# Hyena convolutions: 1024-wide pipelined combinations, the context's parts spread over the layer, and the Fourier products inside the second inverse transform

## The chip, the cores and the metric

The kernel runs on one core of one Trainium2 chip. The metric is the time of one execution on the device in microseconds (us), the median of several runs. Engines are named as in the profile: PE is the matrix engine (TensorE), DVE VectorE, ACT ScalarE, POOL GpSimd, SP the engine whose queue issues most loads.

## The reference

Two layers of a diffusion backbone over 1024 latent tokens and 256 context tokens, width 1024, in float32. Every layer ends with a gated FFN, and each part is modulated by six vectors per layer (shift, scale and gate, twice) that come from the conditioning vectors by `silu(cond) @ ada_w + ada_b`. Layer 1 is neighbourhood attention; layer 0 is the mixer that the change is about:

```
def mixer_ab(u, ...):                       # 1024 latent tokens, and again 256 context tokens
    p = u @ w_in                            # 1024 -> 2048 columns
    y_f = fourier_mix(p[..., :512])         # real part of a 2-D FFT in 4 groups of 128 channels
    y_h = hyena_mix(p[..., 512:], ...)
    return concatenate([y_f, y_h], -1) @ w_out

def hyena_mix(p, ...):
    z = short_conv(p, conv_w, conv_b)       # 3 taps
    x1, x2, v = split(z, 3)                 # 512 channels each
    v = x1 * long_conv(v, filt[:, 0], skip[0])
    v = x2 * long_conv(v, filt[:, 1], skip[1])
    return v                                # long_conv: rfft of length 2L, product, irfft, + skip
```

Both branches run for the latent tokens and for the context tokens with the same weights.

## The kernel before, in words

All matrices are multiplied in a split form: an operand is rounded to a 32-bit matrix format, `hi`, by ACT (`split`, L326), DVE forms the rest, `lo = x - hi` (L328), and three products, hi x hi, lo x hi and hi x lo, are added up in PSUM. So each tile that DVE or PE made costs a copy on ACT and a subtraction on DVE before PE can use it. Programs are written as Python generators that are advanced by hand (`next`), and a scheduler turns what they emit into one in-order queue for each engine. Buffers come from rotating pools: `S4` (128x1024), `S2`, `T`, `TK` and `G` (128x512), in PSUM `PS` (six banks) and `PQ` (two). In the profile `S4` and `S2` tiles are called `s`, the pools `T`, `TK`, `G` are `t`, `tk`, `g`, the banks `ps` and `pq`, matrices of the transforms `mat` (loaded as `cs`), DRAM scratch `d`.

Layer 0 goes through these stages:

- `in_proj` (L821) multiplies by `w_in` in 16 blocks. Between its blocks run `ada_group` (six modulation vectors; here m = 2 to 5, two steps per block, on DVE at L507) and the transforms of the context's filters.
- `turned` (L932) transposes the latent operand into eight blocks.
- The first long convolution is eight `unit(0, fb, cls)` (L967): products with a transform matrix give two PSUM banks, the real and imaginary spectrum of 128 frequencies by 512 channels. A unit of class 0 has 12 matmuls, one of class 1 has 24, in two halves. `combine` (L904) then multiplies by the filter's spectrum: for each of the two parts DVE makes two products (L919 and L920), POOL adds or subtracts them (L921), and ACT and DVE split the sum into Y.
- `inverse_first` (L1000) transforms back in four groups of products (j, r), and DVE and POOL form from them, with the gate x1, the operands of the second convolution (L1025 to L1046).
- Eight `unit(1, fb, cls)` follow; three of them have their first halves ahead of the end of `inverse_first`. Then `inverse_last` (L1053) transforms back and applies x2.
- `fourier_l` (L1253) is the second half of the latent Fourier mix, and `out_proj` (L1338) multiplies by `w_out`.
- The context's own parts (`fourier_c`, `forward_c(0)`, `inverse_c(0)`, `forward_c(1)`, `inverse_c(1)`) form one chain, `ctx_chain`, advanced one step at a time while `inverse_first`, the units and `inverse_last` run; its products use `pq`.

Of the kernel before, what the change touches and what calls it, by code (L numbers as in the profile page):

```python
# [18 lines left out]
P = 128  # L19
D = 1024  # L20
KB = D // P
# [10 lines left out]
PAD_C, PAD_T, SLOT, SHIFT = 24, 88, 1088, 16  # L32
# [204 lines left out]
class Builder:  # L237
    def __init__(self, ctx, tc, a, out, taps=None, stop=None):
# [4 lines left out]
        self.p4 = ent(tc.tile_pool(name="p4", bufs=20))  # L243
        self.p2 = ent(tc.tile_pool(name="p2", bufs=35))
        self.pg = ent(tc.tile_pool(name="pg", bufs=4))
        self.pt = ent(tc.tile_pool(name="pt", bufs=7))
# [99 lines left out]
    def weights(self, src, w=1024, cut=False, keep=None, wide=False, load=None):  # L346
        st = self.S4() if wide else self.W("ws", "ws")
        if keep:
            hi, lo = keep
        else:  # L350
            hi, lo = self.pair3() if wide == 3 else self.pair1() if wide == 2 else self.pair2()
        (load or self.ld)(st.rearrange("p (n k) -> p n k", n=4) if cut else st[:, :w], src)
        self.split(st[:, :w], hi[:, :w], lo[:, :w])
        return hi, lo
# [466 lines left out]
    def in_proj(self, u, fill):  # L821
# [14 lines left out]
        for nb in order:  # L836
            wh, wl = self.weights(a["w_in"][nb])
            acc = self.lin(wh, wl, 0, range(KB), u, PCS)
            for g, n in fill:
                for _ in range(n):  # L840
                    next(g, None)
            if nb < 4:
# [18 lines left out]
            else:  # L861
# [11 lines left out]
                t = self.S2(F32, 256)  # L873
# [4 lines left out]

    def forward_c(self, o):
        nc, a = self.nc, self.a  # L880
        ab = self.ab["c"]
        tr = []
        for j in (0, 1):
            ps = self.PQ()
            for cb in range(4):
                nc.tensor.transpose(ps[:, cb * P:(cb + 1) * P], ab[cb][:, j * P:(j + 1) * P], self.ident)
            hi, lo = self.S2(F32R), self.S2(F32R)
# [3 lines left out]
        for cls in (0, 1):  # L891
            spec = []
            for i in (cls, 2 + cls):
                xh, xl = tr[(i + i // 2) % 2]
                mt = self.cmat(256, a["vf_c"][i, 0])
                ps = self.PQ()
# [4 lines left out]
            self.combine("c", o, cls, 0, spec)  # L901
            yield

    def combine(self, sq, o, cls, fb, spec):  # L904

        nc = self.nc
        Y = self.Y.setdefault((sq, o), {})
        d = self.frg[(sq, o, cls, fb)]
        fr, g = self.TK(), self.TK()
# [3 lines left out]
        if cls == 0 and fb == 0:  # L913
            fr2 = self.S2()
            self.ld(fr2, d[2])
        c, s = spec
        for kind, (x0, x1, op) in enumerate((((c, fr), (s, g), SUB), ((c, g), (s, fr2), ADD))):
# [4 lines left out]
            if sq == "l":  # L922
                key = (kind, cls, fb // 2)
                if key not in Y:
                    Y[key] = (self.S4(F32R), self.S4(F32R))
                hi, lo = (q[:, (fb % 2) * 512:(fb % 2) * 512 + 512] for q in Y[key])
            else:
                hi, lo = self.S2(F32R), self.S2(F32R)
                Y[(kind, cls, 0)] = (hi, lo)
            self.split(t0, hi, lo)  # L930

    def turned(self):  # L932
# [3 lines left out]
        for j in range(8):  # L936
# [6 lines left out]
            if j == 5:  # L943
                self.xrow = [self.S4() for _ in range(4)]
                self.xrev = []
                for cb in range(4):
                    x = self.xrow[cb]
                    self.ld(x, self.xd[0][cb][:, :LAT])
                    t = self.S2()
                    nc.scalar.copy(t.rearrange("p (j c) -> p j c", c=256),  # L950
                                   x.rearrange("p (j h c) -> p j h c", h=2, c=256)[:, :, 1, ::-1])
                    self.xrev.append(t)
            yield

    def turn_x(self, k):

        j, h = k // 4, k % 4
        n0 = (j, j, 4 + j, 2 + j)[h]
        ps = self.PQ()
        for cb in range(4):  # L960
            x = (self.xrev if h % 2 else self.xrow)[cb][:, n0 * P:n0 * P + P]
# [3 lines left out]
        self.xt[(j, h)] = t  # L965

    def unit(self, o, fb, cls):  # L967
# [13 lines left out]
        spec = [self.PS(), self.PS()]  # L981
# [11 lines left out]
        self.combine("l", o, cls, fb, spec)  # L993
        yield

    def y_of(self, o, i, f):
        kind, cls = (0, i) if i < 2 else (1, i - 2)
        return (q[:, (f % 2) * 512:(f % 2) * 512 + 512] for q in self.Y[("l", o)][(kind, cls, f // 2)])

    def inverse_first(self, ahead):  # L1000

        nc, a = self.nc, self.a
        V, G = nc.vector, nc.gpsimd
        new = [None] * 8
        for j in (0, 1):
# [27 lines left out]
            late = V if j else G  # L1033
            V.tensor_tensor(w0, c0, d0, ADD)
            V.tensor_tensor(d0, c0, d0, SUB)
# [4 lines left out]
            V.tensor_tensor(c0, w0, d0, ADD)  # L1040
            V.tensor_tensor(w0, w0, d0, SUB)
            late.tensor_tensor(c1, w1, d1, ADD)
            late.tensor_tensor(w1, w1, d1, SUB)
            p, q = self.TK(), self.TK()
            for k, (dst, x, y, op) in enumerate(((p, c0, c1, ADD), (c0, c0, c1, SUB), (q, w0, w1, ADD), (w0, w0, w1, SUB))):
                V.tensor_tensor(dst, x, y, op)  # L1046
                hi, lo = self.S2(F32R), self.S2(F32R)
                self.split(dst, hi, lo)
                new[(0, 4, 2, 6)[k] + j] = (hi, lo)
# [3 lines left out]
    def inverse_last(self, y):  # L1053

        nc, a = self.nc, self.a
        C, x = [], []
        for r in (0, 1):
            acc = [self.PS() for _ in range(4)]
            first = set()

            def product(cb, m, e, i, f):
                yh, yl = (q[:, cb * P:cb * P + P] for q in self.y_of(1, i, f))
                d = acc[cb][:, e * 256:e * 256 + 256]
                for k, (s, w) in enumerate(((yh, m[:, :256]), (yh, m[:, 256:]), (yl, m[:, :256]))):
                    nc.tensor.matmul(d, s, w, start=cb not in first, stop=e == 1 and i == 1 and f == 3 and k == 2,
                                     skip_group_check=True)
                    first.add(cb)

# [1393 lines left out]
```

## Time and profile before

| what | us |
|---|---|
| median of 3 runs (2949.43 to 2956.27) | 2953.89 |
| the profiled execution | 2960.39 |
| its span in the trace | 2957.4 |
| PE busy | 2832.0 |
| DVE busy | 2097.2 |
| ACT busy | 1328.6 |
| POOL busy | 528.5 |

In the profiled execution the input projection lies from about 255 to 452 us, the convolutions from there to 668, `fourier_l` to 706, and the output projection after it. A row of the profile names the source line, the engine, the operation and the tiles written and read, then how many there were, their busy time and mean length, and how long the engine stood idle ahead of them and for whom.

### The profile page before, as it was taken

To read this page: it belongs to the slowest core of one execution; us is meant where nothing else is said; L and a number is where in the kernel's file an instruction comes from. 1 tells how busy PE (TensorE), PEld (TensorE's weight loads), DVE (VectorE), ACT (ScalarE), POOL (GpSimd) and SP (SyncE) were. 2 spreads that over 40 slices of the span, in tenths; PEclk is the share of its full clock that TensorE was granted. 3 is DMA by queue.
4 is the path that set the end of the run, shared out by engine and by line. 5 is a ranking of instruction groups with operands and counts; after the bars stand their busy time and mean duration, and the time that the engine had idled before them with its cause. 6 is when DMAs were issued, how large, how long until landed. Compare 5 with 4: busy or idle time off the path is not lost. (4 is left out here: it accounts for less than half of the span.)

```text
span 2957.4 us, 44598 instructions
## 1 busy us (share of the span) xinstructions
PE 2832.0 (96%) x15704; PEld 2359.7 (80%) x15704; DVE 2097.2 (71%) x3984; ACT 1328.6 (45%) x2496; POOL 528.5 (18%) x816
## 2 busy tenths in 40 slices
PE   8899999689999999999999999999999999999998
PEld 3678888577899888888888888888877788788886
DVE  6667697676586777876877537788778967664555
ACT  4443325343455333333445326677765533333433
POOL 2112023251110111212010002233212012112000
PEclk9999999899999999999999999999999999999999
DMA  9674446275456555658885435777856266434663
GB/s 335 203 247 160 170 153 198 69 228 183 176 178 207 181 185 191 212 192 296 309 311 176 143 123 144 172 186 180 226 175 230 92 223 230 164 114 162 218 194 135
DMA packets 304813, 567.36 MB, mean 192 GB/s; under 512 B 83528, under 2 KB 130314, under 8 KB 304590
## 3 DMA queue, kind: packets, MB, share of 16 engines
q1 hardware_dynamic: 245950, 380.45, 41.2%
q0 software_dynamic: 56336, 179.87, 17.0%
q10 hardware_dynamic: 2304, 4.20, 0.4%
q8 instruction: 123, 2.02, 0.3%
q14 instruction: 100, 0.82, 0.1%
HBM read 414.44 MB, written 119.80 MB: 181 GB/s over the span
## 5 line engine op out<-in xcount | busy, mean ns | idle before, releaser
L1507 PE MATMUL ps<-s,s 128*128 128x512 f32 x1992 | 494.5, 390 | 5.1 <-DVE s L1398 1.7
L1507 PEld LDWEIGHTS ps<-s,s 128*128 128x128 f32 x1992 | 374.0, 188 | 84.5 <-ACT g L1512 2.1
L322 PE MATMUL ps<-s,wh 128*128 128x256 f32 (+1 forms) x1768 | 394.5, 329 | 2.7 <-ACT wh L326 2.7
L322 PEld LDWEIGHTS ps<-s,wh 128*128 128x128 f32 x1768 | 295.0, 190 | 37.8 <-ACT wh L326 5.1
L322 PE MATMUL pq<-s,wh 128*128 128x512 f32 (+1 forms) x984 | 300.4, 382 | 6.7 <-DVE s L1904 3.2
L326 ACT CAST wh<-ws 128x1024 fp32r<-128x1024 f32 (+1 forms) x142 | 145.8, 1028 | 307.7 <-PE ps L322 172.9
L1678 PE MATMUL ps<-s,s 128*128 128x512 f32 (+1 forms) x1000 | 259.3, 383 | 3.8 <-DVE s L328 3.7
L328 DVE TENSOR_TENSOR wl<-ws,wh 128x1024 fp32r<-128x1024 f32 (+1 forms) x142 | 170.4, 1201 | 128.7 <-ACT wh L326 124.1
L322 PE MATMUL ps<-s,wl 128*128 128x256 f32 (+1 forms) x884 | 256.7, 328 | 2.6 <-DVE wl L328 2.6
L326 ACT CAST s<-s 128x1024 fp32r<-128x1024 f32 (+2 forms) x184 | 168.4, 941 | 197.5 <-DMA s<-d 174.1
L322 PE MATMUL ps<-s,s 128*128 128x64 f16 (+3 forms) x2669 | 221.8, 236 | 18.6 <-DVE st L1976 8.5
L326 ACT CAST s<-t 128x512 fp32r<-128x512 f32 (+1 forms) x242 | 140.3, 591 | 199.9 <-PE ps L1507 65.8
L328 DVE TENSOR_TENSOR s<-t,s 128x512 fp32r<-128x512 f32 (+1 forms) x242 | 172.4, 723 | 77.0 <-ACT s L326 45.0
L328 DVE TENSOR_TENSOR s<-s,s 128x1024 fp32r<-128x1024 f32 (+2 forms) x162 | 185.0, 1176 | 58.3 <-ACT s L326 58.0
L1678 PEld LDWEIGHTS ps<-s,s 128*128 128x128 f32 x1000 | 184.6, 188 | 41.5 <-DVE s L328 5.1
L322 PE MATMUL ps<-s,mat 128*128 128x512 f32 x732 | 191.5, 411 | 25.8 <-ACT s L326 17.7
L322 PEld LDWEIGHTS pq<-s,wh 128*128 128x128 f32 x984 | 178.8, 190 | 39.8 <-DVE s L1904 5.0
L322 PEld LDWEIGHTS ps<-s,mat 128*128 128x128 f32 x732 | 142.0, 198 | 63.9 <-ACT s L326 20.2
L1507 PE MATMUL ps<-s,wh 128*128 128x512 f32 x608 | 189.4, 390 | 0.0
L322 PE MATMUL pq<-s,wl 128*128 128x512 f32 (+1 forms) x492 | 183.7, 380 | 0.0
L322 PEld LDWEIGHTS ps<-s,wl 128*128 128x128 f32 x884 | 164.2, 190 | 20.4 <-DVE wl L328 3.7
L313 POOL DMA_DIRECT2D d<-s x153 | 83.0, 544 | 391.9 <-DVE s L1356 116.5
(434 smaller groups left out, 5566.5 us busy)
## 6 DMA issues: line engine op xcount, KB each, us to landing
s<-d SPq DMA_DIRECT2D x282, 256.0 KB, 3.8
s<-in_down SPq DMA_DIRECT2D x150, 256.0 KB, 4.2
d<-s POOLq DMA_DIRECT2D x137, 256.0 KB, 2.8
d<-tk POOLq DMA_DIRECT2D x98, 256.0 KB, 3.1
s<-in_ada_w POOLq DMA_DIRECT2D x48, 512.0 KB, 4.7
g<-in_bias SPq DMA_DIRECT2D x128, 192.0 KB, 2.9
ws<-in_up SPq DMA_DIRECT2D x44, 512.0 KB, 4.2
d<-g POOLq DMA_DIRECT2D x87, 256.0 KB, 2.7
```

The lines of the kernel that those rows point to most:

```text
L313: self.last_ldr = self.nc.gpsimd.dma_start(out, in_).ins
L322: self.nc.tensor.matmul(o, l, r, start=st, stop=sp)
L326: self.last_hi = nc.scalar.copy(hi, src).ins
L328: self.last_lo = eng.tensor_tensor(lo, src, hi.bitcast(F32), SUB).ins
L1507: nc.tensor.matmul(ps, x[:, sl], y, start=first and j == 0 and x is wh and y is xh, stop=j == 3 and x is wl, skip_group_check=True)
L1678: m = nc.tensor.matmul(acc[j][:, c0:c1], x[:, sl], y[:, xs], start=first and k == 0, stop=last and k == 2, skip_group_check=True)
```

## The change

- `combine` becomes `combine_c` for the context and `combine_l` for the latent tokens. `combine_l` loads both factors as one tile of 1024 columns, makes each pair of products as one DVE operation 1024 wide (reading a PSUM bank twice), leaves the two sums on POOL, and puts the split off until the next unit's products (`parts`), 1024 wide as well.
- `fourier_c` (as `four`) and the start of the context's convolution (as `conv`) run inside `in_proj`, from its blocks 6 and 14 on. The rest of the context's chain stands at fixed places among the units and inside `inverse_last`.
- Of the modulation groups only m = 2 and 3 stay in `in_proj`, one step per block; m = 4 goes into the output projection, m = 5 into layer 0's FFN, three steps per pass.
- The units run in another order, and four instead of three have their first halves ahead.
- `inverse_first` has all its sums on DVE, in an order that finishes the first operands earlier; the gate x1 is loaded in halves (`gate_rows`).
- `fourier_l` is advanced inside `inverse_last`, whose POOL operation goes to DVE. `out_proj` takes its first four column blocks in two halves of the contraction, the Fourier half first.
- Pools: one `S4` more, one `T` less; the scratch for descriptors is halved.

PE's queue at the end of `inverse_first`. `s<-...,mat` rows into `ps` are its products, the `pq` rows are `fourier_c`'s. Before:

```order
L322 MATMUL ps_5290<-s_1231_4692,mat_5298 128x512
L322 MATMUL ps_5290<-s_1232_4693,mat_5298 128x512
L322 MATMUL ps_5290<-s_1231_4692,mat_5298 128x512 x2
L322 MATMUL pq_4923<-s_1274_4861,s_1294_4901 128x256
L322 MATMUL pq_4923<-s_1274_4861,s_1295_4902 128x256
L322 MATMUL pq_4923<-s_1274_4861,s_1294_4901 128x256
L322 MATMUL pq_4929<-s_1282_4869,s_1296_4905 128x256
L322 MATMUL pq_4929<-s_1282_4869,s_1297_4906 128x256
L322 MATMUL pq_4929<-s_1282_4869,s_1296_4905 128x256
L322 MATMUL ps_5290<-s_1232_4693,mat_5298 128x512
```

After, the last products of `inverse_first` (`ps_5234`) and the first of unit (0, 1) of the second convolution (`ps_5289`, `ps_5290`):

```order
L322 MATMUL ps_5234<-s_1261_4832,mat_5243 128x512
L322 MATMUL ps_5234<-s_1262_4833,mat_5243 128x512
L322 MATMUL ps_5234<-s_1261_4832,mat_5243 128x512
L322 MATMUL ps_5234<-s_1272_4869,mat_5243 128x512
L322 MATMUL ps_5234<-s_1273_4870,mat_5243 128x512
L322 MATMUL ps_5234<-s_1272_4869,mat_5243 128x512
L322 MATMUL ps_5289<-s_1337_5163,mat_5285 128x512
L322 MATMUL ps_5290<-s_1335_5159,mat_5287 128x512
```

The `pq` rows have left this part of the queue; they stand among the blocks of the input projection.

DVE's queue at the first combinations of the second convolution. Before, unit (0, 0) (`ps_5344`, `ps_5345`), among splits of the context's (`s_1463`, `s_1467`), and the start of unit (0, 1):

```order
L919 TENSOR_TENSOR t_5510<-ps_5344,tk_5504 128x512
L920 TENSOR_TENSOR t_5511<-ps_5345,tk_5505 128x512
L919 TENSOR_TENSOR t_5519<-ps_5344,tk_5505 128x512
L328 TENSOR_TENSOR s_1463_5486<-t_5480,s_1462_5485 128x512
L328 TENSOR_TENSOR s_1467_5495<-t_5489,s_1466_5494 128x512
L328 TENSOR_TENSOR s_1474_5516<-t_5510,s_1473_5515 128x512
L920 TENSOR_TENSOR t_5520<-ps_5345,s_1470_5508 128x512
L919 TENSOR_TENSOR t_5564<-ps_5396,tk_5560 128x512
L920 TENSOR_TENSOR t_5565<-ps_5397,tk_5561 128x512
```

After, units (0, 1), (1, 1) and (2, 1):

```order
L949 TENSOR_TENSOR s_1395_5408<-ps_5289,s_1394_5407 128x1024
L956 TENSOR_TENSOR s_1396_5409<-ps_5290,s_1394_5407 128x1024
L949 TENSOR_TENSOR s_1402_5440<-ps_5313,s_1401_5439 128x1024
L956 TENSOR_TENSOR s_1403_5441<-ps_5314,s_1401_5439 128x1024
L972 TENSOR_TENSOR s_1405_5448<-s_1395_5408,s_1404_5447 128x1024
L949 TENSOR_TENSOR s_1412_5484<-ps_5333,s_1411_5483 128x1024
L956 TENSOR_TENSOR s_1413_5485<-ps_5334,s_1411_5483 128x1024
L972 TENSOR_TENSOR s_1415_5492<-s_1402_5440,s_1414_5491 128x1024
```

A unit's four products and two splits became two and one, and a unit's split stands behind the next unit's products.

SP's queue in the second convolution's units: `d` rows into `tk` (before) or into 128x2x512 (after) are the factors, `cs` rows transform matrices. Before:

```order
L307 DMA tk_5638<-d_1167 128x512
L307 DMA tk_5639<-d_1167 128x512
L307 DMA cs_5732<-in_vi_c 128x512
L307 DMA tk_5688<-d_1318 128x512
L307 DMA tk_5689<-d_1318 128x512
L307 DMA cs_5812<-in_vfo_l 128x2048
```

After (`d_1663` is a row of `fourier_l`'s operands):

```order
L307 DMA s_1401_5439<-d_1318 128x2x512
L307 DMA s_1537_6033<-d_1663 128x512
L307 DMA cs_5495<-in_vfe_l 128x1024
L307 DMA cs_5528<-in_vfe_l 128x1024
L307 DMA cs_5638<-in_vke_l 128x2048
L307 DMA s_1411_5483<-d_1322 128x2x512
L307 DMA cs_5744<-in_vko_l 128x2048
L307 DMA s_1420_5513<-d_1163 128x2x512
L307 DMA cs_5750<-in_vko_l 128x2048
```

Each factor is one row now, and stands behind matrices of `inverse_last` (`vke`, `vko`) and operands of `fourier_l`, which were loaded later before.

The diff's core:

```
+    def combine_l(self, o, cls, fb, spec):
+        d = self.frg[("l", o, cls, fb)]
+        two = lambda t: t.rearrange("p (e c) -> p e c", e=2)
+        both = lambda t: t.unsqueeze(1).to_broadcast([P, 2, 512])
+        F, t0, t1 = self.S4(), self.S4(), self.S4()
+        self.ld(two(F), d[0:2].rearrange("e p c -> p e c"))
+        c, s = spec
+        nc.vector.tensor_tensor(two(t0), both(c), two(F), MUL)
+        ...
+            last = nc.vector.tensor_tensor(two(t1), both(s), two(F)[:, ::-1], MUL).ins
+        nc.gpsimd.tensor_tensor(t0[:, :512], t0[:, :512], t1[:, :512], SUB)
+        nc.gpsimd.tensor_tensor(t0[:, 512:], t0[:, 512:], t1[:, 512:], ADD)
+        self.parts(last)
+        self.sums_due = (o, cls, fb, t0)
+
+    def parts(self, after=None):
+        if self.sums_due is None:
+            return
+        o, cls, fb, t = self.sums_due
+        self.sums_due = None
+        hi, lo = self.S4(F32R), self.S4(F32R)
+        self.Y.setdefault(("l", o), {})[(cls, fb)] = (hi, lo)
+        self.nc.scalar.copy(hi, t)
+        with self.follow(after):
+            self.nc.vector.tensor_tensor(lo, t, hi.bitcast(F32), SUB)
 ...
     def in_proj(self, u, fill, four, conv):
 ...
+            if i > 5:
+                next(four, None)
+            if i > 13:
+                next(conv, None)
 ...
     def inverse_first(self, ahead):
 ...
-            late = V if j else G
             V.tensor_tensor(w0, c0, d0, ADD)
             V.tensor_tensor(d0, c0, d0, SUB)
-            G.tensor_tensor(w1, c1, d1, ADD)
-            G.tensor_tensor(d1, c1, d1, SUB)
-            for eng, k, w in ((V, 0, w0), (V, 2, d0), (late, 3, w1), (late, 1, d1)):
-                eng.tensor_tensor(w, w, self.xt[(j, k)], MUL)
+            V.tensor_tensor(w1, c1, d1, ADD)
+            V.tensor_tensor(d1, c1, d1, SUB)
+            for k, w in ((0, w0), (2, d0), (3, w1), (1, d1)):
+                V.tensor_tensor(w, w, self.xt[(j, k)], MUL)
 ...
+            sums(c0, c1, (w0, d0), (w1, d1), ADD, p, 0, 4)
+            sums(w0, w1, (w0, d0), (w1, d1), SUB, q, 2, 6)
 ...
+    def inverse_last(self, y, fl):
+        ...
+        next(fl)
         for r in (0, 1):
 ...
+            if r == 0:
+                next(fl)
+            else:
+                for _ in fl:
+                    yield
 ...
     def out_proj(self, wname, y, groups, h, l, m, after, fill):
+        todo = [(g, k, nb) for g, pcs in enumerate(groups)
+                for k, nb in ([(k, nb) for k in (0, 1) for nb in (0, 2)] + [(2, nb) for nb in range(4, KB)] if g == 0 else
+                              [(2, nb) for nb in range(KB)])]
 ...
-        ada = (x for m in (2, 3, 4, 5) for x in self.ada_group(0, m, (0, 1), "s2"))
+        ada = (x for m in (2, 3) for x in self.ada_group(0, m, (0, 1), "s2"))
-        self.in_proj(u, ((filt, 1), (ada, 2)))
+        self.in_proj(u, ((filt, (1,)), (ada, (1,))), fc, cc)
 ...
-        for k in range(8):
-            for _ in self.unit(0, k // 2, k % 2):
+        for k, (fb, cls) in enumerate(((0, 1), (0, 0), (1, 1), (1, 0), (2, 1), (3, 1), (2, 0), (3, 0))):
+            for _ in self.unit(0, fb, cls):
 ...
-        units = [self.unit(1, k // 2, k % 2) for k in range(8)]
-        for _ in self.inverse_first(units[:3]):
-            next(cc, None)
+        units = [self.unit(1, fb, cls, self.PQ if k == 3 else None)
+                 for k, (fb, cls) in enumerate(((0, 1), (1, 1), (2, 1), (0, 0), (1, 0), (3, 1), (2, 0), (3, 0)))]
+        for _ in range(2):
+            next(cc)
+        for _ in self.inverse_first(units[:4]):
+            pass
 ...
-        for i, _ in enumerate(self.inverse_last(y)):
-            if i % 2 == 0:
-                next(cc, None)
-            if i in (2, 6):
-                next(fl)
+        for i, _ in enumerate(self.inverse_last(y, self.fourier_l(y))):
+            next(cc, None)
 ...
-        self.out_proj("w_out", y, [(2, 0), (1,)], h, 0, 2, after1)
+        self.load_cond()
+        self.out_proj("w_out", y, [(2, 0), (1,)], h, 0, 2, after1, self.ada_group(0, 4, (0, 1), "s4"))
 ...
-    nc = _bacc.Bacc("TRN2", target_bir_lowering=False, num_devices=1, dynamic_dma_scratch_size=4096)
+    nc = _bacc.Bacc("TRN2", target_bir_lowering=False, num_devices=1, dynamic_dma_scratch_size=2048)
```

More of the change, by code (lines that the diff above doesn't have):

```diff
@@ L835, in in_proj @@
         next(front)
-        for nb in order:
+        for i, nb in enumerate(order):
             wh, wl = self.weights(a["w_in"][nb])
@@ L1050, in inverse_first, with product @@
+            sums(c0, c1, (w0, d0), (w1, d1), ADD, p, 0, 4)
+            sums(w0, w1, (w0, d0), (w1, d1), SUB, q, 2, 6)
             self.tr = new
             yield
-    def inverse_last(self, y):
+    def inverse_last(self, y, fl):
         nc, a = self.nc, self.a
-        C, x = [], []
+        V = nc.vector
+        C, x, late = [], [], []
+        def product(acc, first, cb, m, e, i, f):
+            yh, yl = (q[:, cb * P:cb * P + P] for q in self.y_of(1, i, f))
+            d = acc[cb][:, e * 256:e * 256 + 256]
+            for k, (s, w) in enumerate(((yh, m[:, :256]), (yh, m[:, 256:]), (yl, m[:, :256]))):
+                nc.tensor.matmul(d, s, w, start=cb not in first, stop=e == 1 and i == 1 and f == 3 and k == 2,
+                                 skip_group_check=True)
+                first.add(cb)
+        next(fl)
```

307 lines of the change are left out of this document (176 added, 131 removed).

## The prediction

> **What bounds the kernel now.** I read the page first, then the windows by stage, then in the stage that loses time the groups of TensorE, its waits, and the timeline of VectorE.
>
> ```profile
> PE 2832.0 (96%) x15704; PEld 2359.7 (80%) x15704; DVE 2097.2 (71%) x3984; ACT 1328.6 (45%) x2496; POOL 528.5 (18%) x816
> 255.00:452.00 197.00, 195.97 (x1018) 165.80 (x1017) 165.83 (x468) 55.57 (x97) 30.38 (x39) 0.99 0.51 175
> 452.00:706.00 254.00, 212.01 (x1108) 178.53 (x1107) 187.88 (x355) 120.16 (x206) 97.44 (x100) 0.91 0.53 169
> 452.00:500.00 48.00, 46.04 (x228) 38.20 (x227) 40.69 (x62) 31.94 (x49) 23.67 (x21) 0.96 0.58 180
> 526.00:575.00 49.00, 26.66 (x119) 20.88 (x118) 38.14 (x98) 14.76 (x39) 12.89 (x11) 0.75 0.12 36
> 575.00:629.00 54.00, 41.98 (x179) 32.94 (x179) 45.53 (x66) 26.47 (x39) 25.28 (x23) 0.91 0.58 186
> 629.00:668.00 39.00, 38.89 (x317) 37.88 (x315) 24.12 (x47) 19.99 (x34) 21.88 (x31) 1.00 0.87 267
> 668.00:706.00 38.00, 32.44 (x153) 26.99 (x153) 34.61 (x70) 14.66 (x28) 10.10 (x12) 0.87 0.67 234
> 850.00:900.00 50.00, 50.00 (x444) 50.00 (x443) 41.01 (x52) 27.30 (x39) 4.88 (x9) 1.00 0.63 197
> 950.00:1000.00 50.00, 50.00 (x222) 41.39 (x222) 42.45 (x85) 20.11 (x33) 7.61 (x14) 1.00 0.52 174
> ```
>
> The columns are stretch, length, then busy time and count of PE, its weight loads, DVE, ACT and POOL, then TensorE's clock, DMA share and GB/s. TensorE is busy 96% of the span, and both versions issue the same matmuls, so the change can only win or lose time in which TensorE does not run at its pace. That pace stands in the last two rows: 50 us for 222 matmuls of 512 columns is 225 ns each, and 50 us for 444 of 256 columns is 113 ns each, with weight loads busy throughout; so I take 113 ns for every narrower one too. Almost everywhere PE fills its stretch. The exception is 452 to 706 us, the long convolutions of the latent tokens, which the change rewrites. Its 512-wide groups:
>
> ```profile
> L322 PE MATMUL ps<-s,mat 128*128 128x512 f32 x432 | 111.6, 416 | 18.6 <-ACT s L326 11.2 <-DVE t L920 2.8 <-DVE t L919 2.1
> L322 PE MATMUL ps<-s,s 128*128 128x512 f32 x63 | 19.1, 454 | 0.0
> L322 PE MATMUL pq<-s,mat 128*128 128x512 f32 x24 | 6.7, 401 | 2.0 <-ACT mat L374 2.0
> L322 PE MATMUL pq<-s,s 128*128 128x512 f32 x21 | 5.1, 389 | 0.0
> ```
>
> 540 of the 1108 matmuls are 512 wide: 540 x 0.225 + 568 x 0.113 = 185.7 us of work in 254 us, so **68 us are lost**, 42 as idle time (254 - 212) and 26 to matmuls that ran slowly between waits (clock 0.91). For the two worst stretches, the 512-wide rows are these, the first from 526 to 575, the others from 575 to 629:
>
> ```profile
> L322 PE MATMUL ps<-s,mat 128*128 128x512 f32 x43 | 13.1, 454 | 11.8 <-ACT s L326 11.2 <-DVE t L1026 0.6
> ...
> L322 PE MATMUL ps<-s,mat 128*128 128x512 f32 x119 | 33.5, 443 | 17.2 <-ACT s L326 10.4 <-DVE t L920 2.8 <-DVE t L919 2.1
> L322 PE MATMUL pq<-s,mat 128*128 128x512 f32 x12 | 3.4, 409 | 2.0 <-ACT mat L374 2.0
> ```
>
> 526 to 575: 43 x 0.225 + 76 x 0.113 = 18.3, lost 31. 575 to 629: 131 x 0.225 + 48 x 0.113 = 34.9, lost 19. The remaining 18 lie in the other stretches. Who is waited for (us in total, times, longest):
>
> ```profile
> PE ps L322 <- ACT s L326: 11.2, 2, 10.4
> PE pq L322 <- DVE s L328: 5.5, 5, 3.3
> PE pq L322 <- ACT s L326: 5.1, 2, 4.8
> ```
>
> The `pq` rows are fourier_c's products: they stand in PE's queue among inverse_first's and the first units', and PE waits there for splits of VectorE. The 10.4 us are the start of units(1), which waits for the last sums of inverse_first. VectorE's timeline before it (start, length):
>
> ```profile
> 562.78 1.40 DVE L1034 TENSOR_TENSOR g<-t,t 128x512 f32<-128x512 f32 x1
> 564.34 1.51 DVE L1035 TENSOR_TENSOR t<-t,t 128x512 f32<-128x512 f32 x1
> 569.52 1.28 DVE L328 TENSOR_TENSOR s<-pq,s 128x512 fp32r<-128x512 f32 x2
> 574.92 0.69 DVE L1046 TENSOR_TENSOR g<-g,g 128x512 f32<-128x512 f32 x1
> ```
>
> **The change part by part.** *Fourier_c and forward_c(0) go into the input projection.* The 31 us of 526 to 575 then lose their cause but for the tail. VectorE has to take this work in 255 to 452, where it is busy 165.8 of 197 us. All it did from 526 to 575, 38.1 us, bounds what comes in. Two of the four modulation groups leave; all four are mainly these rows:
>
> ```profile
> L507 DVE CUSTOM_DVE_ANT_0 s<-s,s 128x512 f32<-128x512 f32 x56 | 39.2, 702 | 0.0
> L507 DVE CUSTOM_DVE_ANT_0 t<-s,s 128x512 f32<-128x512 f32 x42 | 32.0, 773 | 5.4 <-DMA s<-in_ada_w 5.3
> L507 DVE CUSTOM_DVE_ANT_0 tk<-s,s 128x512 f32<-128x512 f32 x13 | 10.5, 810 | 2.1 <-DMA s<-in_ada_w 2.1
> ```
>
> 81.7 us, half of it 41. So VectorE stays at 163 of 197 or below. The matmuls can still arrive before their operands; between nothing and the 21 us that the same work costs today (31 less the tail's 10), I take 3, because blocks of the projection stand between them where now nothing does. Its small loads (128x128) come with it into SP's queue; the 32 modulation loads of the two moved groups leave that queue, and 16 return on POOL's, in the output projection, where they delay nothing that PE waits for.
>
> *The tail of inverse_first.* GpSimd's eight operations move to VectorE and the sums are reordered; after the last product VectorE has some 18 operations of 0.69 us, 12.4 us, before units(1) can use a result. Now 24 first-half matmuls (5.4 us) stand ahead of the second halves. Idle 7 (now 10.4); with the split of the last combination of units(0), which stands behind ten small context operations, 2.5 more.
>
> *The combination.* It is now four 512-wide products, two GpSimd operations and two splits per unit. In units(1), from the timeline and the groups:
>
> ```profile
> 601.16 1.27 POOL L921 TENSOR_TENSOR t<-t,t 128x512 f32<-128x512 f32 x1 [1.23 <-DVE t L920]
> 601.61 1.38 DVE L328 TENSOR_TENSOR s<-t,s 128x512 fp32r<-128x512 f32 x1
> 603.73 1.28 POOL L921 TENSOR_TENSOR t<-t,t 128x512 f32<-128x512 f32 x1 [1.29 <-DVE t L920]
> 604.11 1.45 DVE L328 TENSOR_TENSOR s<-t,s 128x512 fp32r<-128x512 f32 x1
> L919 DVE TENSOR_TENSOR t<-ps,tk 128x512 f32<-128x512 f32 x32 | 21.7, 678 | 1.2 <-PE ps L322 1.2
> L328 DVE TENSOR_TENSOR s<-tk,s 128x512 fp32r<-128x512 f32 x4 | 2.7, 685 | 0.0
> L328 DVE TENSOR_TENSOR s<-s,s 128x1024 fp32r<-128x1024 f32 (+2 forms) x162 | 185.0, 1176 | 58.3 <-ACT s L326 58.0
> ```
>
> A split takes 0.69 alone and about 1.4 when GpSimd's operation is running, and ends 0.55 to 0.56 after it. The cycle is 2.5 us (603.73 less 601.16 is 2.57), 5.1 per unit, against 144 matmuls x 0.225 / 8 = 4.05 for PE: VectorE and GpSimd set the pace. Now a unit costs VectorE three wide operations. The wide product from PSUM is in no row; two narrow ones are 1.36, the wide split 1.18, so 3.5 to 3.9 per unit, plus what GpSimd holds up: nothing to 1.3 us. I take 4.4, and because PE has four units begun and runs on into inverse_last's early products, a loss of 5 in units(1) besides its start. The page "SBUF — State Buffer" of the Trainium skill (section "Specifications (TRN2)") says that a VectorE operation with two SBUF inputs and a GpSimd operation that reads SBUF exclude each other, each for its whole instruction. The two timeline pairs agree with it: the split goes on for its own length after GpSimd's end. The rule speaks against a wide split, which would hold GpSimd for 1.2 us where a narrow one holds it for 0.7; by it the sum would lie between mine and the first rival's.
>
> *The end of the section.* 629 to 706 loses some 13 us today, in fourier_l's dependent steps and two waits for loads. Now fourier_l stands inside inverse_last, and the output projection starts with its Fourier half, 4 blocks, so the tail of inverse_last has cover; 3 to 5 remain, I take 5. Without that cover the price is today's. The x loads start later.
>
> *Elsewhere.* The two moved groups cost 41 us of VectorE, in the output projection and layer 0's FFN (42.45 of 50 us busy): hidden, from 0 to 5 us, taken as 3. Load conditions, pool sizes and the smaller descriptor scratch I cost at 0, at worst a few us.
>
> Sum of what is lost after: 452 to 500, 4 as now; the last combination 2.5; the tail 7; units(1) 5; the end 5; input projection 3; elsewhere 3; slow matmuls after these waits 2.5: 32. Today 68, so **36 us less**. The profiled execution took 2960.4 us, so 2924; it is 6.5 above the median of 2953.9, on which I predict **2918**.
>
> **The rivals.** *The combination's cycle stays (2930).* If GpSimd's two halves, 2.6 us, never overlap the wide split, and the next products follow it, a unit is 2.4 + 1.2 + 1.3 = 4.9 or more and units(1) and units(0) keep their loss: 5 becomes 17. For it: each split quoted above overlapped such an operation. Against: the split now comes a unit later and the products, which read PSUM, can run beside GpSimd. The lock of the Trainium skill's page "SBUF — State Buffer" (section "Specifications (TRN2)") would make it so wherever the split finds GpSimd at work. Chance 0.18.
>
> *The factor loads come late (2942).* The factors F are now one 512 KB transfer behind matrix loads in SP's queue:
>
> ```profile
> tk<-d SPq DMA_DIRECT2D x18, 256.0 KB, 2.7
> s<-d SPq DMA_DIRECT2D x4, 512.0 KB, 6.4
> cs<-in_vfo_l SPq DMA_DIRECT2D x2, 512.0 KB, 3.8
> ```
>
> Today they are two of 2.7 us. In units(1) all but the first stand behind vke, vko or Fourier loads, which wait for a buffer that PE or VectorE frees; when one is issued only then, its unit waits 3.8 to 6.4 us. For five of them at 4.8 that is 24 us. Against: the factors of a unit are needed four units after its first half. Chance 0.12.
>
> *Slower (2972).* The Fourier work stalls PE inside the input projection. PE takes its queue in order; fourier_c has two dependent steps per group and forward_c(0) three, 11 waits. If each finds half a projection block of VectorE work queued ahead (165.8 / 16 blocks / 2 = 5.2 us), that is 57 in place of 3, and 36 of gain become 18 of loss. It decides above 3.5 us per wait. For it: just these steps cost 21 us today, with VectorE less busy. Against: work of the projection stands between. Chance 0.12.
>
> *All of it (2904)*: the tail's wait is covered and units(1) run at PE's pace, 14 us more. Chance 0.10. *No change*, gain lost in many small waits: 0.03.
>
> **How the numbers follow.** My forecast has 0.45. Faster by over 0.2% (6 us, about what a measurement can tell from no change) is 0.45 + 0.18 + 0.12 + 0.10 = 0.85, same 0.03, slower 0.12. The unknown costs move the forecast by 0 to 18 for the Fourier work, 0 to 12 for the combination, a few for the tail; the range from 2896 to 2950 holds the cases on the faster side and leaves out the slower one.
>
> **What would show it.** Right: no wait of `pq` products between inverse_first's, PE at pace from the first unit to inverse_first's end, one gap of 6 to 9 us ahead of units(1), units at 4.1 to 4.6 us. Wrong: PE below 195 us in the 197 of the input projection, or idle time in units(1) that ends at "DMA s<-d", or at combine's products again and again.

## The result, and the profile after

The changed kernel takes 2955.47 us (median of 20 runs, 2949.36 to 2964.18) against 2953.83 for the kernel before (20 runs): ratio 1.0004, 95% interval 0.9996 to 1.0012. Forecast were 2918 us; measured is no change. The profiled execution took 2957.89 us, its span is 2956.0. So 36 us of gain were not there, or were given back. The windows of the changed kernel from the input projection to the output projection (columns as above):

```profile
255.00:456.00 201.00, 190.72 (x995) 161.47 (x994) 134.77 (x367) 60.17 (x125) 34.80 (x48) 0.97 0.40 132
456.00:496.00 40.00, 31.91 (x163) 26.66 (x162) 26.33 (x52) 17.18 (x33) 7.38 (x7) 0.91 0.36 119
496.00:575.00 79.00, 76.89 (x372) 64.04 (x371) 58.57 (x79) 41.14 (x53) 32.27 (x28) 1.00 0.53 169
575.00:625.00 50.00, 38.43 (x177) 31.04 (x176) 33.40 (x36) 20.53 (x22) 21.92 (x13) 0.93 0.66 228
625.00:672.00 47.00, 46.27 (x317) 42.41 (x317) 28.07 (x53) 22.79 (x40) 22.00 (x30) 1.00 0.63 205
672.00:696.00 24.00, 24.00 (x158) 21.92 (x157) 20.98 (x45) 9.51 (x17) 5.38 (x9) 1.00 0.78 286
```

The convolutions are faster: TensorE has no stretch left like 526 to 575 of before (26.7 busy of 49), and the output projection starts at about 696 in place of 706. But in the input projection, where TensorE was busy for 196.0 of 197 us before, it is now busy for 190.7 of 201, and for 31.9 of the 40 us behind it.

To see the whole program, I took from each trace the time between the starts of neighbouring matmuls, less 226 ns for one of 512 columns and 113 for one of 256 (narrower ones by their own usual pace), and added it up between points at which every kernel has done the same amount of matmul work. This is what TensorE loses in each stage, in us. A column is one execution, so a row carries noise: in the first row, kernels with the same code at that place lie between 54.8 and 58.6.

| stage | before | after | e1 | e4 | e5 | e6 | e9 | e10 | e11 | e12 |
|---|---|---|---|---|---|---|---|---|---|---|
| ahead of the input projection | 57.9 | 56.1 | 56.5 | 54.9 | 58.2 | 54.9 | 55.6 | 54.8 | 58.6 | 58.1 |
| input projection | 9.9 | 24.7 | 9.7 | 8.2 | 9.7 | 21.4 | 7.7 | 7.7 | 21.0 | 7.7 |
| its end, first convolution | 5.0 | 16.2 | 5.0 | 11.7 | 3.4 | 16.1 | 26.3 | 26.0 | 17.3 | 17.2 |
| end of inverse_first, units(1) | 50.4 | 13.2 | 44.7 | 45.4 | 47.1 | 13.1 | 13.8 | 13.2 | 15.6 | 12.4 |
| inverse_last, Fourier, start of out_proj | 14.6 | 10.5 | 13.3 | 8.8 | 13.8 | 15.7 | 9.2 | 17.2 | 16.7 | 17.7 |
| out_proj, context's FFN | 10.9 | 14.9 | 11.5 | 16.7 | 11.4 | 14.0 | 12.6 | 16.8 | 15.7 | 16.9 |
| layer 0's FFN, layer 1's start | 10.6 | 12.3 | 11.1 | 10.2 | 10.2 | 14.3 | 12.4 | 14.2 | 11.7 | 13.8 |
| layer 1's attention | 74.9 | 91.0 | 72.5 | 96.1 | 93.7 | 69.5 | 91.7 | 75.2 | 92.7 | 72.6 |
| the rest | 12.0 | 6.4 | 5.3 | 5.1 | 5.9 | 5.3 | 5.2 | 5.3 | 6.6 | 5.2 |

Three rows undo the gain of 41 in the fourth and fifth: 15 in the input projection, 11 at its end, and 16 in layer 1's attention, a stage whose source the change does not touch. In the attention the same 4554 matmuls take 600 us in the kernel before (first row) and 616 in the changed one:

```profile
1764.00:2364.00 600.00, 565.01 (x4554) 479.55 (x4554) 479.50 (x1110) 393.00 (x1053) 137.12 (x199) 0.99 0.63 175
```

```profile
1752.00:2368.00 616.00, 572.48 (x4554) 483.26 (x4553) 484.05 (x1108) 394.22 (x1054) 137.11 (x199) 0.98 0.60 171
```

The work is the same, and most of the difference is waiting of one engine for another. One operation takes longer itself: VectorE's sum of two softmax parts. Its row, and the wait that costs ScalarE most, in the kernel before first, then in the changed one:

```profile
L1982 DVE TENSOR_TENSOR st<-st 128x2 f32<-128x2 f32 x64 | 17.7, 276 | 16.4 <-ACT g L1981 16.0
ACT t L1979 <- DVE st L1978: 48.9, 32, 3.3
```

```profile
L2081 DVE TENSOR_TENSOR st<-st 128x2 f32<-128x2 f32 x64 | 27.2, 424 | 29.8 <-ACT g L2080 29.3
ACT t L2078 <- DVE st L2077: 68.3, 46, 5.6
```

The sum takes about 0.155 us by itself and 0.64 to 0.75 on average where it overlaps GpSimd's 1.17 us subtraction of the same stage (L1991 before, L2090 after). That happens to 16 of the 64 sums in the kernel before and to 29 in the changed one, and makes up the nearly 10 us that VectorE spends longer on this row.

TensorE's waits in the changed kernel, inside the input projection, at its end, and (two rows) in the second convolution's units:

```profile
PE ps L322 <- ACT s L326: 5.2, 6, 1.6
...
PE pq L1006 <- DVE s L816: 6.1, 1, 6.1
...
PE ps L322 <- DVE s L949: 4.6, 1, 4.6
PE ps L322 <- ACT s L326: 4.4, 2, 3.9
```

The first row is fourier_c's products, six waits in the projection (whose window shows a clock of 0.97); four smaller rows of waits there add 4.8 us. The second is one wait of 6.1 us for a PSUM bank, and the timeline shows why (start, length):

```profile
477.20 0.68 DVE L934 TENSOR_TENSOR t<-ps,s 128x512 f32<-128x512 f32 x1
478.71 1.08 DVE L328 TENSOR_TENSOR s<-t,s 128x512 fp32r<-128x512 f32 x1 [0.84 <-ACT s L326]
480.60 0.56 ACT L814 ACTIVATE s<-pq,c 128x256 f32<-128x256 f32 x1
481.85 0.48 DVE L816 SCALAR_TENSOR_TENSOR s<-pq,c,s 128x255 f32<-128x255 f32 x1
482.48 1.09 PE L1006 MATMUL pq<-c,g 128*128 128x128 f32 x4 [6.09 <-DVE s L816]
```

The bank holds the projection's last block. Its eviction (L814, L816) stands on ScalarE and VectorE behind forward_c(0)'s combination (L934, L328), and the next matmuls in TensorE's queue need that bank.

The new combination itself, by VectorE's and GpSimd's groups from 496 to 625, and two splits with GpSimd beside them:

```profile
L972 DVE TENSOR_TENSOR s<-s,s 128x1024 fp32r<-128x1024 f32 x14 | 21.1, 1505 | 3.9 <-ACT s L970 3.8
L949 DVE TENSOR_TENSOR s<-ps,s 128x1024 f32<-128x1024 f32 x14 | 17.1, 1221 | 20.2 <-PE ps L322 11.1 <-DMA s<-d 7.4 <-PE pq L1006 1.7
L956 DVE TENSOR_TENSOR s<-ps,s 128x1024 f32<-128x1024 f32 x13 | 15.8, 1213 | 0.1
L958 POOL TENSOR_TENSOR s<-s,s 128x512 f32<-128x512 f32 x14 | 25.0, 1789 | 0.0
```

```profile
598.91 1.30 POOL L957 TENSOR_TENSOR s<-s,s 128x512 f32<-128x512 f32 x1 [3.38 <-DVE s L956]
599.51 2.00 ACT L374 CAST mat<-cs 128x1024 fp32r<-128x1024 f16 x2
599.63 1.65 DVE L972 TENSOR_TENSOR s<-s,s 128x1024 fp32r<-128x1024 f32 x1 [0.81 <-ACT s L970]
600.16 2.27 POOL L958 TENSOR_TENSOR s<-s,s 128x512 f32<-128x512 f32 x1
```

A wide product is 1.22 us, a split 1.5: 3.9 us of VectorE's work per unit. From one unit's first product to the next one's it is 4.8 and 4.6 us at the end of units(1) (starts at 615.93, 620.70 and 625.28), where the cycle was 5.1 before. Earlier in units(1) there are waits for the factors, because SP's queue stood ahead of them at matrix loads that wait for ScalarE's casts of earlier matrices (575 to 625):

```profile
DVE s L949 <- DMA s<-d: 7.0, 2, 3.5
SPq L307 <- ACT mat L388: 18.8, 3, 10.5
```

The later of L949's two waits holds up TensorE as well: its 4.6 us for L949, shown above, end with the product that started 3.5 us late.

### The profile page after: what moved, and what is told of

It is laid out like the page before. It is cut to its first block, busy times and chain, and to the rows that moved or that the text cites. A ratio compares the mean times of both kernels' runs of the same rounds, so it can differ in the third digit from the quotient of the medians.

```text
span 2956.0 us, 44485 instructions
## 1 busy us (share of the span) xinstructions
PE 2832.5 (96%) x15704; PEld 2363.7 (80%) x15704; DVE 2092.7 (71%) x3950; ACT 1330.1 (45%) x2490; POOL 529.2 (18%) x820
## 5 line engine op out<-in xcount | busy, mean ns | idle before, releaser
L322 PE MATMUL ps<-s,wh 128*128 128x256 f32 (+1 forms) x1584 | 358.7, 329 | 3.5 <-ACT wh L326 3.4
L322 PE MATMUL pq<-s,wh 128*128 128x512 f32 (+1 forms) x1040 | 316.2, 381 | 9.8 <-DVE s L1990 4.7
L322 PEld LDWEIGHTS ps<-s,wh 128*128 128x128 f32 x1584 | 265.8, 192 | 29.6 <-ACT wh L326 4.7
L322 PE MATMUL ps<-s,s 128*128 128x64 f16 (+3 forms) x2780 | 243.8, 241 | 31.1 <-DVE s L2099 8.8
L328 DVE TENSOR_TENSOR wl<-ws,wh 128x1024 fp32r<-128x1024 f32 (+1 forms) x142 | 170.0, 1198 | 127.5 <-ACT wh L326 123.0
L322 PE MATMUL ps<-s,wl 128*128 128x256 f32 (+1 forms) x792 | 238.4, 327 | 2.7 <-DVE wl L328 2.7
L326 ACT CAST s<-t 128x512 fp32r<-128x512 f32 (+1 forms) x213 | 121.9, 587 | 220.9 <-PE ps L1605 81.2
L328 DVE TENSOR_TENSOR s<-s,s 128x1024 fp32r<-128x1024 f32 (+2 forms) x162 | 185.5, 1177 | 49.4 <-ACT s L326 46.9
L322 PE MATMUL ps<-s,mat 128*128 128x512 f32 x714 | 180.3, 402 | 18.1 <-ACT s L326 10.9
L322 PE MATMUL pq<-s,wl 128*128 128x512 f32 (+1 forms) x520 | 196.3, 379 | 1.3 <-DVE wl L328 1.3
L328 DVE TENSOR_TENSOR s<-t,s 128x512 fp32r<-128x512 f32 (+1 forms) x213 | 136.9, 653 | 78.9 <-ACT s L326 51.0
L322 PEld LDWEIGHTS ps<-s,mat 128*128 128x128 f32 x714 | 135.6, 193 | 54.9 <-ACT s L326 13.5
L322 PEld LDWEIGHTS ps<-s,s 128*128 128x128 f32 (+1 forms) x860 | 133.9, 196 | 45.3 <-ACT s L326 10.9
L322 PEld LDWEIGHTS ps<-s,wl 128*128 128x128 f32 x792 | 148.8, 191 | 16.4 <-DVE wl L328 3.6
```

The costliest lines, as they stand in the source:

```text
L322: self.nc.tensor.matmul(o, l, r, start=st, stop=sp)
L326: self.last_hi = nc.scalar.copy(hi, src).ins
L328: self.last_lo = eng.tensor_tensor(lo, src, hi.bitcast(F32), SUB).ins
```

## The experiments

All totals are medians, ratios are to the kernel before on the same chip, with 95% intervals.

**e1: one T buffer less in the kernel before.**

```
-        self.pt = ent(tc.tile_pool(name="pt", bufs=7))
+        self.pt = ent(tc.tile_pool(name="pt", bufs=6))
...
-PAD_C, PAD_T, SLOT, SHIFT = 24, 88, 1088, 16
+PAD_C, PAD_T, SLOT, SHIFT = 24, 624, 1088, 16
```

> The kernel before with six T buffers in place of seven and the pad of that pool longer by as much, so that every other buffer keeps its address. Theory A (layer 1's attention needs the seventh T buffer): slower by 12 to 16 us, about 2968, with the loss between the end of layer 0's FFN and the end of the attention. Theory B (the smaller descriptor scratch slows GpSimd's transfers): 2954. Theory C (the order of the attention's instructions is drawn anew by any change ahead of it, with no fixed price): anything from -10 to +16.

2941.03 us, 0.9956 (0.9941 to 0.9971): faster by 13 us. Theory A fell. The attention keeps its 72.5; 6 us come from the end of inverse_first, 7 from the last stage, which loses 9 to 12 in the three kernels with seven T buffers (before, e2, e3) and 5.1 to 6.6 in every other kernel of the table. Why a buffer less helps there I did not follow further.

**e2: the descriptor scratch halved in the kernel before.** `dynamic_dma_scratch_size=4096` becomes 2048.

> The kernel before with the descriptor scratch halved, 4096 to 2048, and nothing else; the order of every engine's instructions stays. Theory B: slower by 10 us or more, GpSimd's transfers landing 0.4 to 0.5 us later. Theories A and C: the same, 2954 within 3.

2954.93 us, 0.9995 (0.9981 to 1.0009). Theory B fell.

**e3: the changed kernel with the pools of before** (20 S4, 7 T, pad 88, scratch 4096).

> The changed kernel with the pools and scratch of before (20 S4, 7 T, pad 88, scratch 4096). Theory A or B: the attention's 16 us come back, about 2940. Theory C: the attention takes some other time than in both, and the total says nothing on T or scratch by itself.

2952.64 us, 0.9989 (0.9973 to 1.0005). The attention lost 78.4, so most of its 16 us came back, but the total is 12 above the 2940 of theories A and B; the Fourier and inverse_last stage lost 17.7 in place of 10.5, and the last stage some 3 more.

**e4: the context's chain back where it was.**

```
-        self.in_proj(u, ((filt, (1,)), (ada, (1,))), fc, cc)
+        cc = (x for g in (four(), conv()) for x in g)
+        self.in_proj(u, ((filt, (1,)), (ada, (1,))), iter(()), iter(()))
...
         for _ in self.inverse_first(units[:4]):
-            pass
+            next(cc, None)
...
```

> The changed kernel with the context's chain where it was before: fourier_c and forward_c(0) out of the input projection, one step at each yield of inverse_first, at every second unit and in inverse_last, on the PQ banks. If they are what the input projection and its end lose, 255 to about 480 us gets back 20 us of TensorE's time (lost there: 10 as before in place of 25, and no wait of 6 us at its end), and inverse_first loses some 20 to 31 as before. Rival: the projection's loss comes from its slower filling of modulation and filter steps, and stays at 25 without the context's products.

2964.49 us, 1.0033 (1.0017 to 1.005). The input projection:

```profile
255.00:442.00 187.00, 186.29 (x977) 157.51 (x976) 129.49 (x312) 54.15 (x96) 30.51 (x39) 1.00 0.41 140
```

TensorE is busy throughout again, and the end of inverse_first loses 45.4 in place of 13.2. So the move of the context's chain is what wins 32 us there, and it pays 16.5 in the projection and 4.5 at its end. The other 7 us at the projection's end are not the context's.

The traces show the order of each engine's instructions. VectorE's 768 and ScalarE's 785 instructions of the attention's items stand in one order in before, e1, e2 and e3, and in another in after and e4. The first four have 20 S4 buffers, the others 21. The later runs keep to this: e6, e8, e10 and e12, with 20, have the first order, and e5, e7, e9 and e11, with 21, the second.

**e5: the kernel before with the pools of the change.**

```
-        self.p4 = ent(tc.tile_pool(name="p4", bufs=20))
+        self.p4 = ent(tc.tile_pool(name="p4", bufs=21))
...
-        self.pt = ent(tc.tile_pool(name="pt", bufs=7))
+        self.pt = ent(tc.tile_pool(name="pt", bufs=6))
...
-PAD_C, PAD_T, SLOT, SHIFT = 24, 88, 1088, 16
+PAD_C, PAD_T, SLOT, SHIFT = 24, 112, 1088, 16
...
-dynamic_dma_scratch_size=4096
+dynamic_dma_scratch_size=2048
```

> The kernel before with the four numbers of the change's pools (21 S4, 6 T, pad 112, scratch 2048). In the programs the attention's instructions on VectorE and ScalarE stand in the same order in this kernel, in the changed one and in e4 (all with 21 S4), and in another order that is the same in before, e1 and e3 (20 S4). Theory D (the 21st S4 buffer gives the attention the other order, and that order costs 16 us): the attention loses about 91 us of TensorE's time in place of 72 to 75, and the total is e1's 2941 plus 16, about 2957. Rival: the loss follows what the changed kernel does ahead of the attention; then this one is at e1's 2941.

2962.88 us, 1.0028 (1.0015 to 1.0041), 22 above e1. The attention's window and VectorE's row in it:

```profile
1758.00:2377.00 619.00, 573.34 (x4555) 484.15 (x4554) 484.02 (x1110) 393.19 (x1053) 137.22 (x199) 0.98 0.60 170
...
L1982 DVE TENSOR_TENSOR st<-st 128x2 f32<-128x2 f32 x64 | 26.8, 419 | 29.8 <-ACT g L1981 29.3
```

With no line of the change but its numbers for pools and scratch, the attention takes on the changed kernel's rows: 93.7 lost, and 29 of the 64 sums overlap GpSimd's subtraction, as there.

**e6: the changed kernel with 20 S4** (T at 6, pad 624, scratch 4096).

> The changed kernel with 20 S4 in place of 21, the T pool at 6, scratch and addresses as in e1. Theory D: the attention loses 72 to 78 in place of 91, total about 2940 (2955.5 less 16), plus what the missing S4 buffer costs in the convolutions (e3 lost 7 more there). Rival: about 2955.

2945.81 us, 0.9965 (0.995 to 0.9981). The attention:

```profile
1754.00:2349.00 595.00, 564.10 (x4556) 479.33 (x4554) 481.16 (x1110) 396.05 (x1053) 137.28 (x199) 0.99 0.62 177
```

Theory D holds from both sides: 21 S4 in the kernel before bring the loss, 20 in the changed one take it away. Over all kernels, 69.5 to 78.4 are lost with 20 S4, and 89.5 to 96.1 with 21. What a buffer less costs is in the same run: the Fourier stage loses 15.7 in place of 10.5. That is one wait, for the output projection's weights (690 to 715):

```profile
PE ps L1438 <- ACT wh L326: 6.8, 1, 6.8
```

The changed kernel with 20 S4 has it in every run (7.1 in e3, 7.8 in e8, 7.5 in e10, 8.0 in e12), the changed kernel itself has not. (e6's profiled execution, 2935.8, lies 10 below its median.)

**e7: forward_c(0) out of the input projection**, into units 0 to 2 of the first convolution.

```
-            if i > 13:
-                next(conv, None)
...
-            if k == 6:
+            if k in (0, 1, 2, 6):
                 next(cc)
```

> The changed kernel with forward_c(0) moved from the last two blocks of the input projection to the first three units of the first convolution. Theory E (TensorE's 6 us wait at the projection's end is for a PSUM bank whose eviction stands on VectorE and ScalarE behind forward_c(0)'s combination): that wait goes, the stretch from the projection's end to inverse_first loses about 9 us in place of 16, total about 2948. The input projection keeps a loss of 20 to 25, as that is fourier_c's. Rival: the wait is for something else and stays; then 2955.

2953.61 us, 0.9999 (0.9982 to 1.0015). The wait of 6.1 us went, as expected, but the stretch lost 14.5, not 9, and the total is the changed kernel's within the noise. TensorE's waits from 456 to 550 are now these:

```profile
PE pq L1004 <- ACT s L1006: 3.2, 1, 3.2
PE ps L322 <- ACT s L365: 2.5, 3, 1.2
PE pq L1004 <- ACT s L326: 1.5, 1, 1.5
PE ps L322 <- DVE s L970: 1.0, 1, 1.0
```

L365 is the cast of forward_c(0)'s matrices, the two rows of L1004 are the gate's transposes, and L970 is the combination's split. The input projection lost 20.8: of the 16.5, some 12.6 are fourier_c's and 4 forward_c(0)'s.

**e8: e6 and e7 together.**

> e6 and e7 together. If both theories hold: about 2932 (2955.5 less 16 less 8), faster than before, the change and e1.

2952.42 us, 0.9995 (0.9982 to 1.0008): a miss by 20. The attention lost 73.2 as it should; the rest is spread over five stages by 2 to 5 us each against e6, and I have no cause for it. The medians of e8 and e6 are only 6.6 us apart, as e6's profiled execution was 10 below its median, so differences of that size in a row are not clear of the noise.

**e9: fourier_c in three steps per group.**

```
             prs = self.folded(p0, p1, P, q[:, g:g + 1], qn[:, g:g + 1], nc.gpsimd)
+            yield
             ae, ao, am = self.channels(prs, cg, 1, self.PS)
+            yield
...
-            if i > 5:
+            if i > 4:
```

> The changed kernel with fourier_c emitted in three steps per group in place of one (operands, channel products, second products), one step per block of the input projection from block 5 on. Theory F (TensorE stands in its queue at fourier_c's dependent products, because product and operand are emitted in one block): the projection loses about 14 in place of 25, total about 2946. Rival: the context's work lengthens the waits of whatever stands next, and the projection stays at 20 to 25.

2949.76 us, 0.9978 (0.9967 to 0.9989). The input projection and TensorE's longest wait behind it (440 to 545):

```profile
255.00:443.00 188.00, 187.33 (x1011) 160.08 (x1010) 131.97 (x354) 61.00 (x122) 36.93 (x50) 1.00 0.43 143
...
PE ps L322 <- ACT s L365: 10.7, 2, 7.7
```

Theory F holds: with a block of the projection between operand and product the projection loses 7.7, less than before the change. But forward_c(0)'s matrices are now waited for 10.7 us, and the next row of the table goes from 16.2 to 26.3. The total is 5.7 below the changed kernel's, 4 above the 2946 expected.

**e10: e9 with 20 S4.**

> e9 with the pools of e6 (20 S4). If theories D and F hold: about 2936, faster than e1 and e6; if F falls, e6's 2946.

2941.45 us, 0.9941 (0.9925 to 0.9958). The attention lost 75.2 and the projection 7.7, as both theories have it; the total is 5 above the 2936 expected.

**e11: narrow operations in the new combination.**

```
-        nc.vector.tensor_tensor(two(t0), both(c), two(F), MUL)
+        for e in (0, 1):
+            nc.vector.tensor_tensor(t0[:, e * 512:e * 512 + 512], c, F[:, e * 512:e * 512 + 512], MUL)
```

(and likewise the second product and the split)

> The changed kernel with every 1024-wide operation of combine_l and its split on VectorE made as two of 512, in the same places. If the width is what brings the units to TensorE's pace: 8 to 12 us slower, about 2965. If what counts is that the split comes a unit later and that fourier_c is gone from the queue: 1 to 4 us slower, about 2958.

2961.35 us, 1.0027 (1.0016 to 1.0038), 6 us above the changed kernel and between the two expectations. VectorE's groups from 496 to 625:

```profile
L975 DVE TENSOR_TENSOR s<-s,s 128x512 fp32r<-128x512 f32 x26 | 36.7, 1448 | 2.1 <-ACT s L972 2.1
L950 DVE TENSOR_TENSOR s<-ps,s 128x512 f32<-128x512 f32 x26 | 16.6, 679 | 14.3 <-PE ps L322 10.1 <-DMA s<-d 4.2
```

The products gain little from width: 2 x 0.68 against 1.22. The split gains much: 2 x 1.45 against 1.5. In 10 of the 13 pairs of narrow splits both halves are lengthened beside operations of GpSimd (0.88 to 1.78 us, against 0.68 alone); of the 14 wide ones six are (1.38 to 2.3, against 1.22). How much of the 6 us this makes stays open: e11's column, from an execution 7 us above its median, is higher by 3.5 in the two rows of the convolutions and by 6.2 in that of inverse_last, for which I have no cause.

**e12: e10 and e7 together.**

> e10 with forward_c(0) moved into the first three units of the first convolution, as in e7. In e10 TensorE waits 10.6 us at the projection's end for forward_c(0)'s matrices (cast by ScalarE after a load on SP's queue). If that wait goes and only e7's small ones appear: about 2934, the fastest of all. If the matrices come as late there: about 2941 as e10.

2936.4 us, 0.9952 (0.9938 to 0.9966); the waits for L365 fell from 10.6 to 2.8. It has the lowest median, but on another chip; its ratio is no lower than e10's, so that moving forward_c(0) won nothing that shows, and its interval overlaps those of e10 and of e1. Three kernels beat both versions by some 0.4 to 0.6%, and which is the fastest isn't settled. e1 does it with two numbers.

## Why the prediction was wrong, point by point

The forecast was 36 us of gain and none came, so some 38 are to be accounted for. Two steps failed. The larger is the price of the context's work at its new place: the sum has 3 for it in the input projection and 2.5 behind, the traces show 15 and 11 (second and third points), 20 of the 38. The other is the pool sizes, with 0 in the sum: 16 in one stage, and 4 to 8 on the total.

- *Pool sizes at 0, at worst a few us*: the 21st S4 buffer gave layer 1's attention another order of instructions, and that order lost 91.0 in place of 74.9 (e5 and e6 show it from both sides). I looked only at the stages that the diff names, and the reading that TensorE fills its stretch almost everywhere but from 452 to 706 passed over the 74.9 that the attention lost already. That the order does the harm, and not the buffer's presence or the addresses that shift with the pools, is argued: all kernels with one order have the same count of S4 buffers. One part of the harm goes with the order in all of them: 16 or 17 of the 64 sums overlap GpSimd's subtraction with the one, 29 with the other. The other pool number, one T buffer less, wins: all the pool and scratch numbers together cost 0.28% (e5), 8 us, on the kernel before, and by e3 some 4 us on the changed one.
- *Fourier work in the input projection, 3 between 0 and 21*: it was 15. Mechanism and bounds were right, the choice between them was not: product and operand came from one step, so the projection's blocks did not stand between them, as the prediction had assumed. e9 puts them there and the loss in the projection is gone, though 10 us come back behind it.
- *452 to 500: 4 as now, and 2.5 for a split*: 16.2. The last block's eviction behind forward_c(0)'s combination was missing (6.1 us in one wait); e7 shows that removing that wait alone wins 1.7, since others take its place.
- *The tail of inverse_first 7, units(1) 5*: 13.2 measured in that row, where 12 were forecast. The move of the context's chain wins 32 there (e4), as read from the waits. That the sum came out so near is in part luck: the tail's wait was 4.4 in place of 7, and up to 4.6 of the rest is the wait behind a late factor load, which the sum did not hold.
- *Cycle 4.4 per unit*: 4.6 to 4.8 where no load is late, of which VectorE's own work is 3.9. Its 1.18 for a wide split is the mean of a row of mixed widths; alone it takes 1.22. The price of the lock was as the timeline had it: in the split and the GpSimd operation quoted above each goes on about 1.1 us after the other's end (601.28 against 600.21, 602.43 against 601.28), some 0.15 less than its length alone, as the prediction's narrow splits went on for 0.55 of their 0.69. The Trainium skill's page "SBUF — State Buffer" has such operations exclude one another for whole instructions; the section that states it is "SBUF: two separate sides", not the one that the prediction names. The prediction's argument against a wide split holds for GpSimd, whose two operations take 1.67 and 1.79 us on average (L957, L958) against 1.29 and 1.64 with narrow ones (e11, L959 and L960); but e11 shows that two half splits cost VectorE more still.
- *The end of the section 5*: 10.5 stand against 14.6 before. One wait of 2.1 us for an eviction of the output projection is in it, and 2.8 us by which inverse_last's 288 matmuls of 256 columns run slower than 113 ns; the rest is in no single wait. *Elsewhere 3*: 5.7 in the two rows behind the output projection's start, about 4 of it by the slower matmuls of the context's FFN (last section).
- *The late factor loads*: they came, twice, at 7.0 us of VectorE's waiting in units(1) ("DMA s<-d" on L949), and with the rival's mechanism, a queue that stands at a matrix load. TensorE lost up to 4.6 us by it, a fifth of the rival's 24.
- *The slower side*: its mechanism was found, at 15 us of its 57. Its sign was there too: TensorE busy for 190.7 of 201 us in the input projection. The outcome is the case of no change, which had 0.03, but by a few large losses, not by many small waits as I had put it.

Summed up: a gain of 41 us in the two rows that were aimed at, in place of 44.5 (the 36, and the 3, 3 and 2.5 that were set against them); 26 given back at the work's new place, against 5.5 allowed; 16 lost in the attention and 6 won in the last stage, neither foreseen, and 6 lost between them, where 3 were allowed. With equal pools the rest of the change is worth little in any setting: 0.9965 (e6) against 0.9956 (e1), 1.0004 against 1.0028 (e5), 0.9989 (e3) against 1. So even without the pools the forecast gain was not there.

## What to carry to other kernels

Where a scheduler sets the order, a pool's size is a change to every stage that uses that pool: compare the instruction order of the untouched stages too, and try the pool numbers by themselves, on both versions, before crediting or blaming the code. Work moved into a saturated stretch must be cut so that one block of that stretch lies between each operand and its product, and so that its last steps do not stand ahead of the stretch's own last evictions. A total that does not move can be a gain and a loss of equal size; adding up TensorE's lost time by equal work shows both.

## What the runs showed of the hardware that was not expected

The context's FFN, 256-wide matmuls with weight loads busy throughout, ran at 113 ns each in the kernel before (444 in 50 us) and at 117 ns in the changed one, from its trace:

```profile
825.00:900.00 75.00, 75.00 (x639) 75.00 (x638) 60.66 (x78) 40.89 (x57) 7.43 (x14) 1.00 0.60 194
```

Neither kernel has a wait there, and the clock is 1.00 in both. Over the 960 matmuls of that stage it makes some 4 us. It is not the pools by themselves: e5, with the new pools and the old code, keeps 113 ns. Nor does it follow the changed code as such, since e9 has the faster pace again, and e10, the same code with e9's 21 S4 made 20, the slower (e9 first, then e10):

```profile
850.00:900.00 50.00, 50.00 (x443) 50.00 (x443) 36.13 (x46) 27.91 (x39) 5.40 (x10) 1.00 0.71 223
```

```profile
850.00:900.00 50.00, 50.00 (x427) 50.00 (x426) 37.25 (x46) 26.69 (x37) 4.87 (x9) 1.00 0.60 200
```

All other runs have one of the same two paces: 113 in e1 and e2, 117 to 118 in e3, e4, e6, e7, e8, e11 and e12. What decides between them stays open.
